# Attention scores in three passes: the lo keys meet only the hi queries over 64 rows, two blocks side by side on the array's halves

## The chip, the cores and the metric

The kernel runs on one core of a Trainium2 chip. The metric is the device time of one execution in microseconds (us). The engines are PE (TensorE, with its weight loads shown apart as PEld), DVE (VectorE), ACT (ScalarE), POOL (GpSimd) and SP (SyncE, which here issues nearly all DMAs).

## What is computed

One layer of a decoder trunk over a sequence of 1024 positions and a model width of 1024, in float32. Three causal token mixers share one normalised input and one wide input projection:

- branch a, differential attention: 4 heads, each with two score maps (m = 0, 1) over 64-wide queries and keys; the weights are the first softmax less lambda times the second;
- branch b, sliding-window attention: 8 query heads over 2 key heads, a window of 128, a sink per head;
- branch c, forgetting attention: 8 heads, with a decay that is a running sum over positions.

```python
s = jnp.einsum('bqhmd,bkhmd->bhmqk', qblk, k) * scale
p = jax.nn.softmax(s + bias[None, :, None], axis=-1)
w = p[:, :, 0] - lam * p[:, :, 1]
...
s = jnp.einsum('bqhd,bkhd->bhqk', qblk, k) * scale
s = jnp.where((dist >= 0)[None, None], s + decay, -jnp.inf)
p = jax.nn.softmax(s, axis=-1)
```

The first three lines are of branch a, the others of c. Each branch is gated, projected up, merged by sigmoid gates, projected once more and added to the input; a last RMSNorm ends the trunk.

## The kernel before

Every float32 operand of a matmul is kept as two parts, hi (rounded to the format that PE reads, float32r) and lo (the rest), and a product is the sum of the part products.

The work goes in stages. First the input is normalised and the value columns are projected. Then the other projections run in pairs of tiles (`strassen`, lines 160 to 211; its matmuls are lines 109 to 111); queries and keys are split by `spill` (line 417) and written to a scratch tensor in memory, `qd[t, row, s]`, with t = 0 for hi and 1 for lo. The attention stage follows (from line 573), then up-projection and output.

In the attention stage PE's order is written by hand: the loop at line 931 goes through 64 parts (16 of branch b, 32 of c, 16 of a). A part of b is one block of 128 queries; a part of c or a is one group g of two query blocks, i = 2g and 2g + 1, with g going 3, 2, 1, 0 in each head. In each round, the scores of part n (list `sa`) are mixed with the transposes (line 671) and output matmuls (lines 704, 775) of part n - 2 (list `tv`) in proportion to their nominal costs, and after every such piece `fill` puts in filler matmuls: three 512-column matmuls of a gate projection (lines 526 to 528) at a time. The other engines are ordered by a scheduler.

**Scores.** A head's query and key vectors have 64 numbers, so hi and lo stand under each other in 128 rows: `load_q` (line 606) loads hi in rows 0 to 63 and lo in 64 to 127; `load_k` (line 609) loads the hi keys into both halves of one tile and the lo keys into both halves of another. `scores` (line 618) makes a block of up to 512 scores with two matmuls of 128 rows: one gives q_hi k_hi + q_lo k_hi, the other q_hi k_lo + q_lo k_lo. A block is at least 256 wide.

**Score tiles.** Each block goes into a PSUM tile `sc` of one bank; there are two such buffers (BS = 2). VectorE reads it once (line 645 in c and a, line 752 in b: bias, scale and running minimum m into the tile e), followed by a short read of the accumulator. ScalarE then makes the exponentials (lines 651, 755), GpSimd normalises (lines 659, 835).

In `part_c` (line 783) the bias of a group is the tile dk. The odd block is done first; then GpSimd masks 128 columns of dk in place (line 809), and the even block reads the same tile.

**Queues.** SP issues the loads of a part three parts ahead (AHEAD = 3). Query and key tiles share one pool, qk, of NQK = 16 buffers.

Of the kernel before, what the change touches and what calls it, by code (L numbers as in the profile page):

```python
# [32 lines left out]
NST, NW, NSF = 5, 4, 4  # L33
NE, NF, NQK = 6, 3, 16
BP, BS, BT, BY = 2, 2, 2, 2
# [14 lines left out]
def hybrid_block_kernel(ctx, tc, x, norm_gain, w_in, b_forget, lambda_q1, lambda_k1, lambda_q2, lambda_k2,  # L50
# [165 lines left out]
    with tc.tile_pool(name="blk", bufs=8) as blk, \  # L216
# [199 lines left out]
        with tc.tile_pool(name="qkp", bufs=2, reuse_waits="tile") as qkp:  # L416
            def spill(row, scale, c, src):
                hi = qkp.tile([P, 512], F32R, name="qk_hi", bufs=3)
                lo = qkp.tile([P, 512], F32R, name="qk_lo", bufs=3)
                if isinstance(scale, float):  # L420
                    nc.scalar.activation(hi, src, AF.Copy, scale=scale)
                else:
                    nc.scalar.activation(hi, src, AF.Identity, scale=scale)
                nc.vector.scalar_tensor_tensor(lo, src, scale, hi.bitcast(F32), ALU.mult, ALU.subtract)
                for t, v in enumerate((hi, lo)):
                    nc.sync.dma_start(qd[t, row * P:row * P + P, c * 512:c * 512 + 512], v.bitcast(F32))

# [16 lines left out]

            def qk(row, scale):
                return lambda c, src: spill(row, scale, c, src)
            tb.update(hb)
# [43 lines left out]
            for hp in range(4):  # L491
                tiles += [(QC + hp * P, qk(hp, SCALE)), (KC + hp * P, qk(4 + hp, 1.0))]
            tiles += [(QB + t * P, qk(16 + t, qscale_b[:, t:t + 1])) for t in range(4)]
# [79 lines left out]
    with tc.tile_pool(name="at", bufs=2, reuse_waits="tile") as at, \  # L573
# [31 lines left out]

        def load_q(row, m):
            return load_rows(row, m, (0, 1))

# [8 lines left out]

        def scores(xq, kk, i, k0, n):

            ps = ps_s.tile([P, 512], F32, name="sc")  # L620
            q = xq[i // 4][:, (i % 4) * P:(i % 4) * P + P]
            c, o = divmod(k0, 512)
            n = max(n, 256)
            for t in range(2):
                nc.tensor.matmul(ps[:, :n], q, kk[t][c][:, o:o + n], start=t == 0, stop=t == 1)  # L625
            return ps

        def s_cost(n):
            return 2 * max(n, 256) / 2400

        def softmax_rows(xq, kk, i, cuts, bias, scale, tag, done):

# [3 lines left out]

            def chunk(k0, n, last):
                ps = scores(xq(), kk(), i, k0, n)
# [4 lines left out]
                m2 = small.tile([P, 1], F32, name="m")  # L643
                m = st_["m"]
                nc.vector.tensor_tensor_reduce(out=e[:, k0:k0 + n], in0=ps[:, :n], in1=bias(k0, n), op0=ALU.add,  # L645
                                               op1=ALU.min, scale=-scale, scalar=1.0e30 if m is None else m,
                                               accum_out=m2)
                st_["m"] = m2
                if last:
# [4 lines left out]
                    done(e, r, den)  # L654
            ends = cuts[1:] + [L]
            return [(s_cost(z - a), lambda a=a, z=z: chunk(a, z - a, z == L)) for a, z in zip(cuts, ends)]

# [74 lines left out]
        def part_b(u, kv, i):  # L732
# [3 lines left out]

            def score(hh):
                h = 4 * kv + hh
                if hh == 0:
# [7 lines left out]
                ps = ps_s.tile([P, 512], F32, name="sc")  # L747
                q = u["q"][hh][i // 4][:, (i % 4) * P:(i % 4) * P + P]
                for t in range(2):
                    nc.tensor.matmul(ps[:, :2 * P], q, u["k"][t][:, k0:k0 + 2 * P], start=t == 0, stop=t == 1)  # L750
                e = st_["e"][hh // 2][:, hh % 2, :W]
                nc.vector.tensor_tensor_reduce(out=e, in0=ps[:, :W], in1=posB[:, 2 * P - W:], op0=ALU.add,
                                               op1=ALU.min, scale=-SLOPES_B[h], scalar=nsink[:, h:h + 1],
                                               accum_out=m4[:, hh:hh + 1])
                nc.scalar.activation(e, e, AF.Exp, bias=m4[:, hh:hh + 1], scale=-1.0, accum_out=d4[:, hh:hh + 1])
                st_["es"].append(e)
                if hh == 3:
                    s4 = small.tile([P, 4], F32, name="s4")
# [11 lines left out]
            def pv(b):  # L770
# [9 lines left out]
            return ([(0.22, lambda hh=hh: score(hh)) for hh in range(4)], [(0.44, lambda b=b: tr(b)) for b in range(nblk)],  # L780
                    [(0.43, lambda b=b: pv(b)) for b in range(nblk)], lambda: None)

        def part_c(u, hp, hh, g):
# [6 lines left out]
            def prep():  # L790

                if "ck" not in u:
# [30 lines left out]
        def part_a(u, h, g):  # L823
# [14 lines left out]
            for i in (2 * g, 2 * g + 1):  # L838
                L = P * (i + 1)
                for m in range(2):  # L840
                    sa += softmax_rows(lambda m=m: u["q"][m], lambda m=m: u["k"][m], i, [0] if i < 4 else [0, 512],
                                       lambda k0, n, L=L: posA[:, S - L + k0:S - L + k0 + n], SLOPES_A[h],
                                       "a%d" % (m + 1), lambda e, r, d, m=m, i=i: done(m, i, e, r, d))

# [26 lines left out]
        def load_b(u, kv):  # L871
# [4 lines left out]
            for t in range(2):  # L876
# [4 lines left out]
                u["k"].append(k)  # L881
            u["q"] = [load_q(16 + 2 * kv + t, m) for t in range(2) for m in range(2)]

# [262 lines left out]
```

## Time and profile before

| | us |
|---|---|
| three runs of the kernel before | 1195.36, 1203.62, 1210.67 |
| their median | 1203.62 |
| the profiled execution's own time | 1201.41 |
| its span, first to last instruction | 1199.3 |
| PE busy | 1155.8 |
| DVE busy | 798.9 |
| POOL busy | 688.9 |
| ACT busy | 591.9 |

The profile is of one execution on one core. Busy time is the time covered by an engine's instructions; the record of a matmul reaches into the next one, so PE's busy time shows where PE stood still, not its rate. The rate is read from the starts in a timeline. A row of a group gives busy time, the mean of one instruction, and after the bar the idle time before them with what ended it.

### The profile page before, as it was taken

To read this page: it belongs to the slowest core of one execution; us is meant where nothing else is said; L and a number is where in the kernel's file an instruction comes from. 1 tells how busy PE (TensorE), PEld (TensorE's weight loads), DVE (VectorE), ACT (ScalarE), POOL (GpSimd) and SP (SyncE) were. 2 spreads that over 40 slices of the span, in tenths; PEclk is the share of its full clock that TensorE was granted. 3 is DMA by queue.
4 is the path that set the end of the run, shared out by engine and by line. 5 is a ranking of instruction groups with operands and counts; after the bars stand their busy time and mean duration, and the time that the engine had idled before them with its cause. 6 is when DMAs were issued, how large, how long until landed. Compare 5 with 4: busy or idle time off the path is not lost. (4 is left out here: it accounts for less than half of the span.)

```text
span 1199.3 us, 18793 instructions
## 1 busy us (share of the span) xinstructions
PE 1155.8 (96%) x5787; PEld 977.3 (81%) x5787; DVE 798.9 (67%) x1655; ACT 591.9 (49%) x1255; POOL 688.9 (57%) x684
## 2 busy tenths in 40 slices
PE   7999999999999999999999999999998999989997
PEld 6999878878778788887888888888877778878885
DVE  7667786766775774321887766767766835564897
ACT  6432334333443443332886666667876842334433
POOL 5056585665754754454555666665767632377652
PEclk8999999999999999999999999999999999999999
DMA  7442386675854643338945465456567359897332
GB/s 242 159 154 80 112 283 201 216 246 158 257 192 138 221 132 106 114 97 244 272 131 173 145 195 176 130 174 174 171 209 221 122 169 325 270 333 299 141 119 92
DMA packets 184531, 221.70 MB, mean 185 GB/s; under 512 B 16280, under 2 KB 116712, under 8 KB 182640
## 3 DMA queue, kind: packets, MB, share of 16 engines
q1 hardware_dynamic: 184288, 219.99, 58.2%
q8 instruction: 46, 0.75, 0.3%
q10 hardware_dynamic: 144, 0.52, 0.1%
q14 instruction: 53, 0.43, 0.1%
HBM read 144.89 MB, written 75.56 MB: 184 GB/s over the span
## 5 line engine op out<-in xcount | busy, mean ns | idle before, releaser
L104 POOL TENSOR_TENSOR w_lo<-w_st,w_hi 128x512 fp32r<-128x512 f32 x130 | 175.4, 1352 | 109.5 <-ACT w_hi L101 99.0
L104 POOL TENSOR_TENSOR w_lo<-w_sf,w_hi 128x512 fp32r<-128x512 f32 x96 | 137.8, 1440 | 107.4 <-ACT w_hi L101 100.6
L111 PE MATMUL pm<-t,w_lo 128*128 128x512 f32 x320 | 128.7, 402 | 5.4 <-POOL w_lo L104 5.4
L109 PE MATMUL pm<-t,w_hi 128*128 128x512 f32 x320 | 128.5, 402 | 2.5 <-ACT w_hi L101 2.5
L110 PE MATMUL pm<-t,w_hi 128*128 128x512 f32 x320 | 127.6, 399 | 0.0
L625 PE MATMUL sc<-qk 128*128 128x512 f32 (+2 forms) x384 | 102.4, 358 | 4.4 <-DVE m L645 3.8
L101 ACT CAST w_hi<-w_sf 128x512 fp32r<-128x512 f32 x96 | 58.9, 616 | 57.5 <-PE pm L110 51.4
L678 DVE TENSOR_TENSOR pt<-tp,pt 128x512 fp32r<-128x512 f32 x102 | 70.1, 687 | 23.5 <-ACT pt L677 22.7
L101 ACT CAST w_hi<-w_st 128x512 fp32r<-128x512 f32 x86 | 52.4, 617 | 62.0 <-PE pm L110 51.1
L111 PEld LDWEIGHTS pm<-t,w_lo 128*128 128x128 f32 x320 | 61.2, 191 | 21.5 <-POOL w_lo L104 7.1
L625 PEld LDWEIGHTS sc<-qk 128*128 128x128 f32 x384 | 64.9, 190 | 16.3 <-DVE m L645 6.8
L109 PEld LDWEIGHTS pm<-t,w_hi 128*128 128x128 f32 x320 | 61.2, 191 | 17.7 <-ACT w_hi L101 3.7
L110 PEld LDWEIGHTS pm<-t,w_hi 128*128 128x128 f32 x320 | 61.4, 192 | 14.5
L677 ACT CAST pt<-tp 128x512 fp32r<-128x512 f32 x102 | 59.4, 583 | 20.1 <-PE tp L671 18.8
L167 DVE TENSOR_TENSOR w_sf<-w_st 128x512 f32<-128x512 f32 x40 | 43.7, 1093 | 36.0 <-DMA w_st<-in_w_in_dram 21.8
L659 POOL TENSOR_SCALAR e_c<-e_c,r 128x1024 f32<-128x1024 f32 (+3 forms) x64 | 47.9, 748 | 24.5 <-DVE r L653 20.1
L651 ACT ACTIVATE e_c<-e_c,m 128x1024 f32<-128x1024 f32 (+3 forms) x64 | 49.9, 780 | 16.0 <-DVE m L645 15.1
L704 PE MATMUL y<-pt,v 128*128 128x256 f32 x336 | 55.4, 290 | 2.1 <-DVE pt L678 1.8
L651 ACT ACTIVATE e_a<-e_a,m 128x896 f32<-128x896 f32 (+7 forms) x64 | 49.6, 776 | 14.9 <-DVE m L645 14.4
L835 POOL TENSOR_TENSOR e_a<-e_a,e_a 128x896 f32<-128x896 f32 (+7 forms) x32 | 47.6, 1490 | 15.3 <-ACT e_a L834 15.1
L704 PEld LDWEIGHTS y<-pt,v 128*128 128x128 f32 x336 | 48.0, 189 | 6.8 <-DVE pt L678 3.2
L104 POOL TENSOR_TENSOR pwl<-ws,pwh 128x512 fp32r<-128x512 f32 x28 | 40.7, 1455 | 19.9 <-ACT pwh L101 14.2
(299 smaller groups left out, 3467.5 us busy)
## 6 DMA issues: line engine op xcount, KB each, us to landing
w_st<-in_w_in_dram SPq DMA_DIRECT2D x126, 256.0 KB, 3.3
qk<-qd SPq DMA_DIRECT2D x224, 128.0 KB, 3.0
wo<-wod SPq DMA_DIRECT2D x14, 1024.0 KB, 9.3
row<-gmd SPq DMA_DIRECT2D x48, 256.0 KB, 5.1
qd<-qk_hi SPq DMA_DIRECT2D x42, 256.0 KB, 4.2
qd<-qk_lo SPq DMA_DIRECT2D x42, 256.0 KB, 3.8
vd<-vt SPq DMA_DIRECT2D x24, 384.0 KB, 2.3
v<-vd SPq DMA_DIRECT2D x9, 1024.0 KB, 8.2
```

The lines of the kernel that those rows point to most:

```text
L101: nc.scalar.copy(hi, src)
L104: return eng.tensor_tensor(lo, src, hi.bitcast(F32), ALU.subtract)
L109: nc.tensor.matmul(ps, w[0][:, k, :], r[0][:, k, :], start=start and k == 0, stop=False)
L110: nc.tensor.matmul(ps, w[0][:, k, :], r[1][:, k, :], start=False, stop=False)
L111: nc.tensor.matmul(ps, w[1][:, k, :], r[0][:, k, :], start=False, stop=stop and k == n - 1)
L625: nc.tensor.matmul(ps[:, :n], q, kk[t][c][:, o:o + n], start=t == 0, stop=t == 1)
L651: nc.scalar.activation(e[:, :L], e[:, :L], AF.Exp, bias=m2, scale=-1.0, accum_out=den)
L659: nc.gpsimd.tensor_scalar(out=e, in0=e, scalar1=r, scalar2=1.0, op0=ALU.mult, op1=ALU.mult)
L677: nc.scalar.copy(pt[:, 0, a:], tp[:, a:])
L678: nc.vector.tensor_tensor(pt[:, 1, a:], tp[:, a:], pt[:, 0, a:].bitcast(F32), ALU.subtract)
L704: nc.tensor.matmul(y[:, :256], l_, r_, start=t == 0 and n == 0, stop=last and n == len(mms) - 1)
L835: nc.gpsimd.tensor_tensor(e1[:, :L], e1[:, :L], e2[:, :L], ALU.add)
```

## The change

- In the changed kernel a score job has a first matmul over 128 rows (the query's hi and lo by hi keys) and a second one over 64 rows: the lo keys by the hi query alone. The product of lo query and lo key is left out.
- `scores` takes two jobs. It makes the two first passes, then the second pass of job 0 on rows 0 to 63 and of job 1 on rows 64 to 127. For this, job 1's query has lo above and hi below (`turn`): in a and b the load of map m = 1 swaps the parts; in c the spill already swaps them for odd blocks of 128 positions, with two DMAs of 512-byte pieces in place of one.
- Blocks come in pairs (`paired`): in b two heads, in a the two maps of one query block, in c the even and the odd query block of one head. The nominal costs are the sums of the two, so the loop that mixes the lists sees pieces twice as long.
- In a, the lo keys of both maps are loaded as one tile of 128 rows for each half of the sequence.
- In c, the even block's mask is made ahead in a tile of its own, dg, and a block that reaches over the mask is read by VectorE in two instructions.
- NQK goes from 16 to 15. BS stays 2.

```diff
-NE, NF, NQK = 6, 3, 16
+NE, NF, NQK = 6, 3, 15
...
-            def spill(row, scale, c, src):
+            def spill(row, scale, c, src, turn=False):
...
-                    nc.sync.dma_start(qd[t, row * P:row * P + P, c * 512:c * 512 + 512], v.bitcast(F32))
+                    dst = [qd[n, row * P:row * P + P, c * 512:c * 512 + 512] for n in (t, 1 - t)]
+                    if not turn:
+                        nc.sync.dma_start(dst[0], v.bitcast(F32))
+                    for o in range(2 if turn else 0):
+                        to, fr = (a.rearrange("p (b o e) -> p b o e", o=2, e=P)[:, :, o, :]
+                                  for a in (dst[o], v.bitcast(F32)))
+                        nc.sync.dma_start(to, fr)
...
-                tiles += [(QC + hp * P, qk(hp, SCALE)), (KC + hp * P, qk(4 + hp, 1.0))]
+                tiles += [(QC + hp * P, qk(hp, SCALE, True)), (KC + hp * P, qk(4 + hp, 1.0))]
...
-        def load_q(row, m):
-            return load_rows(row, m, (0, 1))
+        def load_q(row, m, turn=False):
+            return load_rows(row, m, (1, 0) if turn else (0, 1))
...
-        def scores(xq, kk, i, k0, n):
-
-            ps = ps_s.tile([P, 512], F32, name="sc")
-            q = xq[i // 4][:, (i % 4) * P:(i % 4) * P + P]
+        def scores(jobs):
...
+            pss = [ps_s.tile([P, 512], F32, name="sc") for _ in jobs]
+            for ps, (q, kh, kl, n) in zip(pss, jobs):
+                nc.tensor.matmul(ps[:, :n], q, kh, start=True, stop=False)
+            for j, (ps, (q, kh, kl, n)) in enumerate(zip(pss, jobs)):
+                r = slice(64 * j, 64 * j + 64)
+                nc.tensor.matmul(ps[:, :n], q[r], kl[r], start=False, stop=True)
+            return pss
+
+        def job(xq, kk, i, k0, n):
             c, o = divmod(k0, 512)
             n = max(n, 256)
-            for t in range(2):
-                nc.tensor.matmul(ps[:, :n], q, kk[t][c][:, o:o + n], start=t == 0, stop=t == 1)
-            return ps
+            return (xq[i // 4][:, (i % 4) * P:(i % 4) * P + P],) + tuple(kk[t][c][:, o:o + n] for t in range(2)) + (n,)
...
+                o = 0
+                for w, b in bias(k0, n):
+                    m2 = small.tile([P, 1], F32, name="m")
+                    m = st_["m"]
+                    nc.vector.tensor_tensor_reduce(out=e[:, k0 + o:k0 + o + w], in0=ps[:, o:o + w], in1=b, op0=ALU.add,
+                                                   op1=ALU.min, scale=-scale, scalar=1.0e30 if m is None else m,
+                                                   accum_out=m2)
+                    st_["m"] = m2
+                    o += w
...
+        def paired(first, second):
+
+            def both(a, b):
+                for f, ps in zip((a[2], b[2]), scores([a[1](), b[1]()])):
+                    f(ps)
+            return [(a[0] + b[0], lambda a=a, b=b: both(a, b)) for a, b in zip(first, second)]
...
+                dg = st_["dg"] = at.tile([P, P], F32, name="dg", bufs=2)
+                nc.gpsimd.affine_select(out=dg, in_=dk[:, q0:q0 + P], pattern=[[-1, P]],
+                                        compare_op=ALU.is_ge, fill=NEG, base=0, channel_multiplier=1)
...
-                if i == 2 * g + 1:
-
-                    dk = st_["dk"]
-                    nc.gpsimd.affine_select(out=dk[:, q0:q0 + P], in_=dk[:, q0:q0 + P], pattern=[[-1, P]],
-                                            compare_op=ALU.is_ge, fill=NEG, base=0, channel_multiplier=1)
...
+            def biases(i, k0, n):
+                dk = st_["dk"]
+                if i % 2 or k0 + n <= q0:
+                    return [(n, dk[:, k0:k0 + n])]
+                return [(q0 - k0, dk[:, k0:q0])] * (q0 > k0) + [(P, st_["dg"])]
...
-            sa = []
-            for i in (2 * g + 1, 2 * g):
-                sa += softmax_rows(lambda: u["q"], lambda: u["k"], i, [0] if i < 4 else [0, 512],
-                                   lambda k0, n: st_["dk"][:, k0:k0 + n], 1.0, "c", lambda e, r, d, i=i: done(i, e, r))
...
+            even, odd = (softmax_rows(lambda: u["q"], lambda: u["k"], i, lambda k0, n, i=i: biases(i, k0, n), 1.0, "c",
+                                      lambda e, r, d, i=i: done(i, e, r)) for i in (2 * g, 2 * g + 1))
+            sa = paired(even, odd)
...
-                u["q"][m] = load_q(8 + h, m)
-                u["k"][m] = load_k(12 + h, m)
+                u["q"][m] = load_q(8 + h, m, m == 1)
+                u["k"][m] = [load_rows(12 + h, m, (0, 0))]
+            lo = [None, None]
+            for c in (1, 0):
+                lo[c] = at.tile([P, 512], F32R, name="qk", tag="qk", bufs=NQK)
+                nc.sync.dma_start(lo[c].bitcast(F32), qd[1, (12 + h) * P:(13 + h) * P, c * 512:c * 512 + 512])
```

The change moves instructions on PE and VectorE. In the rows that follow, a line number is that of the kernel the rows are of; behind the arrow stand the moving operand (for scores the keys) and the weights (the queries); tile numbers tell buffers apart, and the last number is the shape of the output.

The first place is on PE, at the first group of branch c (head 0, g = 3). Before, a block's two passes follow each other, and other work stands between the first block and the second:

```order
L625 MATMUL sc_6313<-qk_6054,qk_6045 128x512
L625 MATMUL sc_6313<-qk_6060,qk_6045 128x512
L775 MATMUL y_6293<-pt_6269,v_5027 128x512 x2
L625 MATMUL sc_6325<-qk_6051,qk_6045 128x512
L625 MATMUL sc_6325<-qk_6057,qk_6045 128x512
L526 MATMUL pj_6309<-h00h_87,w_hi_6115 128x512
L527 MATMUL pj_6309<-h00l_88,w_hi_6115 128x512
L528 MATMUL pj_6309<-h00h_87,w_lo_6116 128x512
L671 MATMUL tp_6341<-ident_80,eb_6152 128x128 x2
L671 MATMUL tp_6341<-ident_80,eb_6153 128x128 x2
```

Now:

```order
L631 MATMUL sc_6337<-qk_6070,qk_6061 128x512
L631 MATMUL sc_6338<-qk_6070,qk_6061 128x512
L634 MATMUL sc_6337<-qk_6076,qk_6061 128x512
L634 MATMUL sc_6338<-qk_6076,qk_6061 128x512
L798 MATMUL y_6313<-pt_6284,v_5043 128x512 x2
L533 MATMUL pj_6333<-h00h_87,w_hi_6126 128x512
L534 MATMUL pj_6333<-h00l_88,w_hi_6126 128x512
L535 MATMUL pj_6333<-h00h_87,w_lo_6127 128x512
L694 MATMUL tp_6358<-ident_80,eb_6176 128x128 x2
L694 MATMUL tp_6358<-ident_80,eb_6177 128x128 x2
```

The four matmuls of a pair stand together, the two half passes at line 634 next to each other; the output matmuls (775, now 798), the fillers and the transposes (671, now 694) that stood between single blocks now all stand behind the pair.

The second place is on PE in the last head of branch a, where the second chunk of query block 4 is followed by the first chunk of block 5. Before:

```order
L625 MATMUL sc_9786<-qk_9196,qk_9190 128x256
L625 MATMUL sc_9786<-qk_9202,qk_9190 128x256
L625 MATMUL sc_9795<-qk_9217,qk_9208 128x512
L625 MATMUL sc_9795<-qk_9223,qk_9208 128x512
L526 MATMUL pj_9701<-h01h_89,w_hi_9691 128x512
L527 MATMUL pj_9701<-h01l_90,w_hi_9691 128x512
L528 MATMUL pj_9701<-h01h_89,w_lo_9692 128x512
L625 MATMUL sc_9804<-qk_9214,qk_9208 128x256
L625 MATMUL sc_9804<-qk_9220,qk_9208 128x256
L625 MATMUL sc_9817<-qk_9199,qk_9190 128x512
L625 MATMUL sc_9817<-qk_9205,qk_9190 128x512
```

Now:

```order
L631 MATMUL sc_9851<-qk_9268,qk_9262 128x256
L631 MATMUL sc_9852<-qk_9280,qk_9274 128x256
L634 MATMUL sc_9851<-qk_9286,qk_9262 128x256
L634 MATMUL sc_9852<-qk_9286,qk_9274 128x256
L631 MATMUL sc_9873<-qk_9271,qk_9262 128x512
L631 MATMUL sc_9874<-qk_9283,qk_9274 128x512
L634 MATMUL sc_9873<-qk_9288,qk_9262 128x512
L634 MATMUL sc_9874<-qk_9288,qk_9274 128x512
L533 MATMUL pj_9763<-h11h_93,w_hi_9759 128x512
L534 MATMUL pj_9763<-h11l_94,w_hi_9759 128x512
L535 MATMUL pj_9763<-h11h_93,w_lo_9760 128x512
```

Before, a filler group or output matmuls stood behind every second block; now two pairs follow each other with no other matmul between them, and a filler group stands behind the second.

The third place is on VectorE, in the same group of branch c as the first: the reading of the last chunk of the even block (512 to 895 of its columns). ISA is the reading of a score tile and, with m alone, of the accumulator. Before:

```order
L645 ISA e_c_6352,m_6353<-sc_6349,dk_6220 128x512
L645 ISA m_6353 128x1
L678 TENSOR_TENSOR pt_6346<-tp_6341,pt_6346 128x512
L653 RECIPROCAL r_6332<-den_6330 128x1
L645 ISA e_c_6352,m_6364<-sc_6361,dk_6220,m_6353 128x384
L645 ISA m_6364 128x1
L678 TENSOR_TENSOR pt_6399<-tp_6394,pt_6399 128x512
```

Now:

```order
L660 ISA e_c_6343,m_6372<-sc_6366,dk_6236,m_6344 128x256
L660 ISA m_6372 128x1
L660 ISA e_c_6343,m_6374<-sc_6366,dg_6241,m_6372 128x128
L660 ISA m_6374 128x1
L660 ISA e_c_6346,m_6381<-sc_6367,dk_6236,m_6347 128x512
L660 ISA m_6381 128x1
L669 RECIPROCAL r_6378<-den_6376 128x1
```

The 384 columns of the even block, one reading before, are read as 256 with the bias dk and 128 with the mask dg; the odd block's reading, which came before the even block's, stands behind them.

## Rows read from the trace of the kernel before

**Rows 1.** The page: busy time of each engine, share of the span, instructions.

```profile
PE 1155.8 (96%) x5787; PEld 977.3 (81%) x5787; DVE 798.9 (67%) x1655; ACT 591.9 (49%) x1255; POOL 688.9 (57%) x684
```

**Rows 2.** Stretches: length, PE, PEld, DVE, ACT, POOL busy; clock, DMA share, GB/s.

```profile
100.00:550.00 450.00, 442.16 (x1930) 362.95 (x1929) 286.91 (x338) 170.71 (x292) 274.73 (x200) 0.99 0.55 174
562.00:635.00 73.00, 70.28 (x417) 60.86 (x417) 60.11 (x213) 58.98 (x186) 40.64 (x76) 1.00 0.74 204
635.00:855.00 220.00, 217.30 (x1335) 189.95 (x1334) 157.49 (x485) 147.29 (x326) 140.23 (x213) 1.00 0.58 168
855.00:975.00 120.00, 110.91 (x653) 93.22 (x651) 79.48 (x271) 90.71 (x208) 82.61 (x81) 0.99 0.56 168
```

**Rows 3.** Timeline of PE in branch c: start us, length us, line, matmul.

```profile
706.50 0.39 PE L526 MATMUL pj<-h10h,w_hi 128*128 128x512 f32 x1
...
706.96 0.40 PE L528 MATMUL pj<-h10h,w_lo 128*128 128x512 f32 x1
707.20 0.63 PE L704 MATMUL y<-pt,v 128*128 128x256 f32 x4
707.67 0.97 PE L625 MATMUL sc<-qk 128*128 128x384 f32 x4
```

**Rows 4.** Timeline of PE around a sums matmul (line 862).

```profile
847.59 0.52 PE L625 MATMUL sc<-qk 128*128 128x384 f32 x2
847.95 0.40 PE L862 MATMUL pj<-y,ones 128*2 128x256 f32 x2
848.18 0.68 PE L625 MATMUL sc<-qk 128*128 128x512 f32 x2
```

**Rows 5.** Timeline of PE's weight loads in branch c.

```profile
702.37 0.46 PEld L671 LDWEIGHTS tp<-ident,e_c 128*128 128x128 f32 x4
702.80 0.19 PEld L526 LDWEIGHTS pj<-h10h,w_hi 128*128 128x128 f32 x1
```

**Rows 6.** Groups of matmuls by line and shape: busy us, mean ns, idle before.

```profile
L625 PE MATMUL sc<-qk 128*128 128x512 f32 x192 | 62.1, 406 | 4.4 <-DVE m L645 3.8 <-DMA qk<-qd 0.5
...
L625 PE MATMUL sc<-qk 128*128 128x256 f32 x128 | 26.8, 291 | 0.0
...
L750 PE MATMUL sc<-kb,qk 128*128 128x256 f32 x128 | 25.9, 292 | 2.7 <-DMA qk<-qd 1.7 <-DVE m L752 1.1
...
L625 PE MATMUL sc<-qk 128*128 128x384 f32 x64 | 16.9, 344 | 0.0
```

**Rows 7.** Timeline of PE in branch a.

```profile
900.85 1.04 PE L625 MATMUL sc<-qk 128*128 128x512 f32 x2 [2.81 <-DVE m L645]
901.68 0.63 PE L704 MATMUL y<-ptz,v 128*128 128x256 f32 x2
```

**Rows 8.** Timeline of VectorE in the same stretch.

```profile
900.11 0.68 DVE L645 CUSTOM_DVE_ANT_0 e_a<-sc,posA 128x512 f32<-128x512 f32 x1
...
901.93 0.69 DVE L645 CUSTOM_DVE_ANT_0 e_a<-sc,posA 128x512 f32<-128x512 f32 x1 [0.48 <-PE sc L625]
```

**Rows 9.** Groups of VectorE by line and shape, 562 to 975 us.

```profile
L645 DVE CUSTOM_DVE_ANT_0 e_a<-sc,posA 128x512 f32<-128x512 f32 x40 | 27.4, 686 | 4.2 <-PE sc L625 3.4 <-POOL w_hi L103 0.2
...
L645 DVE DVE_READ_ACCUMULATOR2_ANT m<- 128x1 f32 x192 | 15.8, 82 | 0.1
...
L645 DVE CUSTOM_DVE_ANT_0 e_a<-sc,posA,m 128x256 f32<-128x256 f32 x8 | 3.9, 482 | 2.4 <-PE sc L625 1.9
...
L645 DVE CUSTOM_DVE_ANT_0 e_c<-sc,dk,m 128x128 f32<-128x128 f32 x8 | 2.8, 350 | 1.1 <-POOL e_c L659 0.5 <-PE sc L625 0.3
```

**Rows 10.** Who waited for whom: us in total, times, longest us.

```profile
DVE e_c L645 <- POOL dk L809: 4.1, 2, 3.1
...
ACT qk_hi L421 <- DMA qd<-qk_lo: 4.2, 2, 2.7
```

**Rows 11.** The page, DMA issues: count, KB each, us to landing.

```profile
qd<-qk_hi SPq DMA_DIRECT2D x42, 256.0 KB, 4.2
```

More of the change, by code (lines that the diff above doesn't have):

```diff
@@ L443, in sigm, with qk @@
                 return put
-            def qk(row, scale):
-                return lambda c, src: spill(row, scale, c, src)
+            def qk(row, scale, turn=False):
+                return lambda c, src: spill(row, scale, c, src, turn)
             tb.update(hb)
@@ L616, in load_v, with softmax_rows, chunk @@
             return v
-        def scores(xq, kk, i, k0, n):
-            ps = ps_s.tile([P, 512], F32, name="sc")
-            q = xq[i // 4][:, (i % 4) * P:(i % 4) * P + P]
+        def scores(jobs):
[7 more added lines that the diff above has]
+        def job(xq, kk, i, k0, n):
             c, o = divmod(k0, 512)
             n = max(n, 256)
-            for t in range(2):
-                nc.tensor.matmul(ps[:, :n], q, kk[t][c][:, o:o + n], start=t == 0, stop=t == 1)
-            return ps
+            return (xq[i // 4][:, (i % 4) * P:(i % 4) * P + P],) + tuple(kk[t][c][:, o:o + n] for t in range(2)) + (n,)
         def s_cost(n):
             return 2 * max(n, 256) / 2400
-        def softmax_rows(xq, kk, i, cuts, bias, scale, tag, done):
+        def softmax_rows(xq, kk, i, bias, scale, tag, done):
             L = P * (i + 1)
             st_ = {"m": None}
-            def chunk(k0, n, last):
-                ps = scores(xq(), kk(), i, k0, n)
+            def chunk(ps, k0, n, last):
                 if k0 == 0:
@@ L642, in chunk @@
                 e = st_["e"]
[L643 to L648, printed above, removed]
+                o = 0
[7 more added lines that the diff above has]
+                    o += w
                 if last:
@@ L654, in chunk @@
                     done(e, r, den)
-            ends = cuts[1:] + [L]
-            return [(s_cost(z - a), lambda a=a, z=z: chunk(a, z - a, z == L)) for a, z in zip(cuts, ends)]
+            return [(s_cost(min(512, L - k0)), lambda k0=k0: job(xq(), kk(), i, k0, min(512, L - k0)),
+                     lambda ps, k0=k0: chunk(ps, k0, min(512, L - k0), k0 + 512 >= L)) for k0 in range(0, L, 512)]
+        def paired(first, second):
[3 more added lines that the diff above has]
+            return [(a[0] + b[0], lambda a=a, b=b: both(a, b)) for a, b in zip(first, second)]
         def normalise(e, r):
@@ L735, in part_b, with score @@
             st_ = {}
-            def score(hh):
-                h = 4 * kv + hh
-                if hh == 0:
+            def score(pr):
+                if pr == 0:
                     st_["m"] = small.tile([P, 4], F32, name="m4")
@@ L746, in score @@
                 k0 = max(i - 1, 0) * P
[L747 to L757, printed above, removed]
+                pss = scores([(u["q"][2 * pr + j][i // 4][:, (i % 4) * P:(i % 4) * P + P],)
+                              + tuple(u["k"][t][:, k0:k0 + 2 * P] for t in range(2)) + (2 * P,) for j in range(2)])
+                for j, ps in enumerate(pss):
+                    hh = 2 * pr + j
+                    h = 4 * kv + hh
+                    e = st_["e"][pr][:, j, :W]
+                    nc.vector.tensor_tensor_reduce(out=e, in0=ps[:, :W], in1=posB[:, 2 * P - W:], op0=ALU.add,
+                                                   op1=ALU.min, scale=-SLOPES_B[h], scalar=nsink[:, h:h + 1],
+                                                   accum_out=m4[:, hh:hh + 1])
+                    nc.scalar.activation(e, e, AF.Exp, bias=m4[:, hh:hh + 1], scale=-1.0, accum_out=d4[:, hh:hh + 1])
+                    st_["es"].append(e)
+                if pr == 1:
                     s4 = small.tile([P, 4], F32, name="s4")
@@ L779, in pv @@
                               yd["b"].rearrange("(h e) s -> e h s", e=64)[:, 4 * kv:4 * kv + 4, i * P:(i + 1) * P])
-            return ([(0.22, lambda hh=hh: score(hh)) for hh in range(4)], [(0.44, lambda b=b: tr(b)) for b in range(nblk)],
+            return ([(0.44, lambda pr=pr: score(pr)) for pr in range(2)], [(0.44, lambda b=b: tr(b)) for b in range(nblk)],
                     [(0.43, lambda b=b: pv(b)) for b in range(nblk)], lambda: None)
@@ L839, in part_a @@
                 L = P * (i + 1)
[L840 to L843, printed above, removed]
+                sa += paired(*[softmax_rows(lambda m=m: u["q"][m], lambda m=m: u["k"][m], i,
+                                            lambda k0, n, L=L: [(n, posA[:, S - L + k0:S - L + k0 + n])], SLOPES_A[h],
+                                            "a%d" % (m + 1), lambda e, r, d, m=m, i=i: done(m, i, e, r, d))
+                               for m in range(2)])
             def lhs(kb):
@@ L881, in load_b @@
                 u["k"].append(k)
-            u["q"] = [load_q(16 + 2 * kv + t, m) for t in range(2) for m in range(2)]
+            u["q"] = [load_q(16 + 2 * kv + t, m, m == 1) for t in range(2) for m in range(2)]
         vc = {}
@@ L896, in load_a @@
             for m in range(2):
-                u["q"][m] = load_q(8 + h, m)
-                u["k"][m] = load_k(12 + h, m)
+                u["q"][m] = load_q(8 + h, m, m == 1)
[4 more added lines that the diff above has]
+                nc.sync.dma_start(lo[c].bitcast(F32), qd[1, (12 + h) * P:(13 + h) * P, c * 512:c * 512 + 512])
+            for m in range(2):
+                u["k"][m].append(lo)
         parts = []
```

## Prediction

> **What bounds the kernel now.** I read the busy shares first: TensorE is busy 1155.8 of 1199.3 us, VectorE 799 [rows 1]. Since a share is a mean over stages, the second view is the table by stretch. The change sits in the attention stage: branch b (562 to 635 us), c (635 to 855) and a (855 to 975). There PE is busy 96, 99 and 92% of the stretch, VectorE 82, 72 and 66%, ScalarE 81, 67 and 76%; the granted clock is 1.00 to 0.99, the 2.4 GHz level [rows 2]. So PE sets the time, but in b not by much, and what a matmul costs there must be read from start to start, since records overlap.
>
> That is the third view, the timeline. A 512-column matmul starts 0.233 us after the one before it (three from 706.50 to 707.20), four of 256 columns take 0.47 us, 0.118 each [rows 3], two of 384 take 0.36 us, so 0.18 each [rows 4]: about 0.456 ns a column. The record of one lasts longer, 0.40 us for 512 columns; its last 0.17 us lie under the next one. Weights are loaded for each matmul; a run of four loads takes 0.43 us, 0.108 each [rows 5], so a load hides under any matmul of 256 columns.
>
> The score groups have 192 + 64 + 128 matmuls at line 625 and 128 at line 750 [rows 6]: 512 in 256 tiles, two passes each over 128 rows. What PE waits for there is small: 3.8 us and 1.1 us on VectorE's reading of a score tile [rows 6].
>
> **The second pass on halves.** The removed term is the lo-query by lo-key product; the second pass then needs 64 rows, and two tiles' second passes stand on rows 0 to 63 and 64 to 127. The changed order has 128 pairs, with the same 256 first passes and 256 half passes. If both halves run at once, a pair costs three passes for four, and saves the shorter of its two: in 64 pairs 256 columns (0.118), in 24 pairs 384 (0.176), in 40 pairs 512 (0.233). The widths follow from the code: b has 32 pairs of 256; each of c's eight heads has 256, 384, 512 with 256, and 512 with 384; each of a's four heads has 256 four times, 384 twice and 512 six times. Sum: 7.6 + 4.2 + 9.3 = **21.1 us saved**, 1.8% of 1199. Everything else on PE stays: the same number of fillers, transposes and output matmuls.
>
> Two costs of the half passes are not in the trace, since every matmul there uses 128 rows.
>
> First, two half loads must come in ahead of the second pair of passes. Under a 512 or 384 pass two loads of 0.108 nearly fit; under a 256 pass (0.118) up to 0.10 sticks out, times 64 pairs: 0 to 6.4 us. I take 2, since runs of loads in rows 5 go by without a gap and half loads go to different rows.
>
> Second, the array changes its shape twice a pair, 256 times. The nearest row is the sums matmul at line 862, with 2 weight columns in place of 128: it starts 0.36 us after two 384-column matmuls, its two take 0.23 us and the next 512 starts on time [rows 4]. So narrowing the columns cost nothing; narrowing the rows is bounded by nothing and by an array that empties first, 0.17 us each time, 256 x 0.17 = 43.5 us. I take 0, the row's value, and keep the other end as a rival. The Trainium skill ("TensorEngine Tiling (Array Packing)", Key Properties) says that changing the tiling mode drains TensorE, and counts 128x32 among the modes. The matmuls at line 862 show no such drain; for 64 rows no run here shows it. By the page's rule the sum would be that of the second rival below.
>
> **Two score tiles, two buffers.** There are two PSUM buffers for scores before and after. Before, tile n waits for VectorE's reading of tile n-2: one reading, with a tile and other work between. Now both buffers are filled by one pair, both readings start when the pair ends, and the next pair needs both. The price from rows: a matmul's end lies 0.17 after the next could start; VectorE picks up 0.04 later (PE record 900.85 + 1.04 = 901.89, reading at 901.93 [rows 7, 8]); a reading of 512 takes 0.69, its accumulator read 0.08 [rows 9]; PE starts 0.06 after the reading's end (900.79, then 900.85). Needed until the second buffer: 0.17 + 0.04 + 0.69 + 0.08 + 0.69 + 0.06 = 1.73 us, less the 0.23 in which the next pair's first tile runs: **1.50 us of other PE work between pairs**; 1.28 for 384, 1.1 to 1.2 for 256. Before, one reading needed 0.96.
>
> The order, priced with the starts above, gives the work between pairs: in branch a none at two of 48 places (the second fence shows one), one filler group of 0.70 at nine, 1.03 to 1.40 at six more; short by 9.8 us in sum. In c 11 of 48 are short (six of them have 1.17 where 1.50 is needed), 2.9 us; in b 4, 3.0 us. That is 15.8 us; the same count over the order of before gives 2.7 us, so 13.1 more, with VectorE free at once. It is not: at 66 to 82% busy, half a 0.69 instruction stands in front about three times in four, 0.25 us. With that the sums are 25.2 and 5.4, so 19.9 more; and 5.4 agrees with the 3.8 + 1.1 = 4.9 us that the trace of before has [rows 6]. I take the middle, **16.5 us lost**, mostly in a. Queued behind a waiting score matmul is everything on PE, fillers too, so the wait is on the path.
>
> **The pieces of c.** The even tile no longer waits for the odd one's mask: its mask goes into a tile of its own (dg), and its last stretch is read in two instructions at two of four groups per head, 16 more instructions of about 0.35 + 0.08 us [rows 9], 6.9 us of VectorE. A third of c's pairs have no room: 2 us on PE. What goes is VectorE's 4.1 us wait for POOL's mask [rows 10]; VectorE isn't the bound, so 0.
>
> **DMAs.** Eight of the 42 qd<-qk_hi writes, and eight lo ones, become two each with 512-byte pieces. They lie between 100 and 550 us, where the DMA engines are 55% busy and PE 98% [rows 2], and land in 4.2 us [rows 11]. Their only reader is the attention stage. What they hold up is the qk_hi buffer, for which ScalarE waited 4.2 us in all [rows 10]: between 0 and 16 x 4.2 = 67 us if each landing were doubled and bare, taken at 0 by the wait row. In branch a the lo keys of both maps come in two whole tiles, 24 DMAs fewer; the score matmuls waited 1.7 + 0.5 us for loads [rows 6], so 0 to -2.2, taken as 0. The pool has one buffer fewer (15); in the order the later loads still stand over 12 us of PE work ahead of their use. SP and POOL queues get no new wait.
>
> **Sum**, on the profiled execution (1201.4 us): -21.1 + 2 + 16.5 + 2 = -0.6, so **1201 us**. The median of the three runs is 1203.6, their spread 1195 to 1211, so the profiled run stands 0.2% below the median. 2% (24 us) is about what a measurement of this kernel can tell from no change.
>
> **Rivals.**
> 1. VectorE keeps up, because PE's delays give it room to empty its queue and shortages don't add. For it: VectorE idles 28 to 34% in c and a. Against: the shortages in a are of the order, not of the queue. Gain whole: 1201.4 - 21.1 = 1180 us. Chance 0.12.
> 2. Changing from 128 to 64 rows and back empties the array. Place: both ends of each half pass; price up to 0.17 each, 43.5 us, less 0.17 at the 32 short places where the readings run meanwhile (5.4): 1201 + 38 = 1239 us, slower by 3%. It decides the sign from about 0.1 us a change (26 us). For it: 64 rows are a shape that no row shows. Against: line 862. Chance 0.13.
> 3. The change doesn't do what it says: the halves follow each other. Nothing is saved, the waits stay: 1201.4 + 16.5 + 2 = 1220 us. For it: before has no two matmuls at once. Against: they use different rows, different score tiles. Beside this: the Trainium skill ("TensorE: Matmul & The Clock Gate", Part 3) has matmuls of different row groups start some 4 ns apart, and four 32-row tiles 3.07 times as fast; no run here shows it yet. Chance 0.13.
>
> **How the numbers follow.** The forecast has 0.62. Its own range is 1187 to 1213: waits from 7 (13 less 6 that PE's other waits give back) to 24 (a queue of 0.5 us), pieces 0 to 3, loads 0 to 6. Faster by over 2% (below about 1179) needs the first rival and some luck in the loads: 0.05. Slower by over 2% (above about 1227): most of the second rival, a little of the third: 0.16. Within: 0.79. The range to hold 8 in 10 takes in most of rivals 1 and 3 and a part of 2: 1181 to 1230.
>
> **What would show it.** Right: the two half matmuls of a pair start within some 20 ns of each other, and the next matmul 0.23 us later for 512; the score lines' idle time for VectorE's m rises from 4.9 to over 15 us, most of it in a, and PE's share there falls under 92%. Wrong: half matmuls 0.1 us or more behind the first pass (rival 2), a full pass apart (rival 3), or waits for m still near 5 us (rival 1). If the stretch before 550 us has grown, my zero for the DMAs was wrong.

## The result, and the profile after

| | us |
|---|---|
| kernel after, median of four runs | 1253.03 (1245.07 to 1258.49) |
| kernel before, median of four runs | 1205.36 (1195.36 to 1210.67) |
| ratio | 1.0422, interval 1.0378 to 1.0465 |
| the profiled execution of after | 1245.07, span 1243.3 |

The change makes the kernel 4.2% slower. The forecast was 1201 us with a range up to 1230, so the time lies outside it. The second rival, an array that empties at each change of shape (1239 us, chance 0.13), comes nearest, but emptying is only half of what a change of shape costs here, and the change of shape is only a part of the loss.

Where did the time go? First the table by stretch, for the part before the attention stage and then for the branches b, c and a. A border in the prediction has to be mended for this: it let branch a begin at 855 us [rows 2], but the first score matmul of a stands at 811.7. That touched no term of its sum. With the right borders the kernel before reads (length, busy time of PE, PEld, DVE, ACT, POOL with counts, granted clock, DMA share, GB/s):

```profile
562.00:636.00 74.00, 71.28 (x423) 61.72 (x423) 60.35 (x214) 59.98 (x190) 40.75 (x76) 1.00 0.74 203
636.00:812.00 176.00, 173.52 (x1081) 152.41 (x1080) 123.82 (x371) 113.03 (x252) 113.01 (x186) 1.00 0.56 166
812.00:976.00 164.00, 154.17 (x902) 130.20 (x901) 112.90 (x382) 123.96 (x277) 110.31 (x107) 0.99 0.58 171
```

and the kernel after:

```profile
100.00:550.00 450.00, 443.34 (x1944) 363.43 (x1944) 288.27 (x335) 169.17 (x291) 277.13 (x203) 1.00 0.57 177
556.00:643.00 87.00, 83.43 (x423) 63.09 (x422) 60.45 (x213) 61.30 (x189) 41.31 (x78) 0.96 0.61 170
643.00:842.00 199.00, 191.14 (x1078) 146.56 (x1078) 126.66 (x403) 111.73 (x253) 111.79 (x184) 0.99 0.50 147
842.00:1023.00 181.00, 168.48 (x904) 123.95 (x903) 112.72 (x383) 124.94 (x277) 108.52 (x106) 0.98 0.47 145
```

Branch b takes 13 us more, c 23, a 17: 53 in all. Before the stage nothing has grown (it begins at 556 in place of 562 us), and what follows it is 3 us shorter, so the spans of the two profiled executions differ by 44. The ratio gives 51: the profiled execution of after lies 8 us under the median of the four, with a mean granted clock of 0.985 where the others have 0.978 to 0.982. In the stage the records show PE the same number of matmuls but for one (2405 and 2406), and "busy" 96, 96 and 93% of the three stretches, against 96, 99 and 94% before. PE stands idle for 24 us of them, 15 before; so most of the 53 is not idle time, its matmuls start further apart. As in the prediction, that shows only in a timeline. PE around one pair of branch a (start, length, line, tile, shapes, count):

```profile
981.11 0.63 PE L631 MATMUL sc<-qk 128*128 128x512 f32 x2
981.67 0.50 PE L634 MATMUL sc<-qk 64*128 64x512 f32 x2
982.11 0.50 PE L533 MATMUL pj<-h10h,w_hi 128*128 128x512 f32 x1
982.44 0.40 PE L534 MATMUL pj<-h10l,w_hi 128*128 128x512 f32 x1
982.67 0.40 PE L535 MATMUL pj<-h10h,w_lo 128*128 128x512 f32 x1
```

The two first passes take 0.56 us until the halves start, where two 512-column matmuls take 0.47 [rows 3]: 0.09 more. Both halves together take 0.44 until the next matmul, 0.21 more than the 0.233 of one pass (0.20 in the median of the 512-column pairs and of the 256-column ones), and the two halves of a pair start 3 ns apart. The first filler matmul behind them takes 0.33 (to 982.44), 0.10 more; the next takes 0.23 again. By the medians a visit to the half shape costs 0.09 + 0.20 + 0.10 = **0.39 us**; 128 visits cost 50 us, and the 21.1 us that the halves save don't pay for it.

The timeline of the weight loads says what the 0.10 are. Here around a pair of c, whose second tile had to wait for its buffer (0.28):

```profile
749.31 0.19 PEld L631 LDWEIGHTS sc<-qk 128*128 128x128 f32 x1 [0.28 <-DVE m L660]
749.73 0.19 PEld L634 LDWEIGHTS sc<-qk 64*128 64x128 f32 x2 [0.24 <-issue]
750.16 0.19 PEld L533 LDWEIGHTS pj<-h00h,w_hi 128*128 128x128 f32 x1 [0.24 <-issue]
750.26 0.19 PEld L534 LDWEIGHTS pj<-h00l,w_hi 128*128 128x128 f32 x1
750.50 0.19 PEld L535 LDWEIGHTS pj<-h00h,w_lo 128*128 128x128 f32 x1
```

with PE in the same stretch:

```profile
748.87 0.94 PE L631 MATMUL sc<-qk 128*128 128x512 f32 x2
749.73 0.49 PE L634 MATMUL sc<-qk 64*128 64x512 f32 x2
750.16 0.50 PE L533 MATMUL pj<-h00h,w_hi 128*128 128x512 f32 x1
750.50 0.40 PE L534 MATMUL pj<-h00l,w_hi 128*128 128x512 f32 x1
```

The load for line 534 starts at 750.26, 0.24 before its matmul, under the one at line 533. The loads of line 634 and of line 533 behind it start together with their own matmuls, at 749.73 and 750.16: a load is not pulled ahead over a change of shape, and the 0.10 is that bare load, a load with no matmul running over it. All 256 half loads of this trace start within 0.01 us of their matmul, and so do the loads of all 86 fillers behind a pair. So each change costs 0.09 in which nothing new starts, and 0.10 of load.

The Trainium skill ("TensorEngine Tiling (Array Packing)", Key Properties) says that a change of tiling mode drains TensorE; the trace agrees, with 0.09 us of it at each change (called emptying from here on), and shows the bare load beside it. The Trainium skill ("TensorE: Matmul & The Clock Gate", Part 3) lets matmuls on different rows start some 4 ns apart; here it is 3 ns.

The waits in the stage, PE's and its loads' (total us, times, longest); the answer to [rows 6]:

```profile
PEld sc L634 <- issue: 19.7, 63, 0.7
PEld pj L533 <- issue: 12.5, 52, 0.4
PEld sc L631 <- DVE m L660: 11.7, 27, 1.0
PEld y L727 <- DVE pt L701: 8.2, 17, 0.8
...
PE pj L888 <- ACT gr L539: 4.5, 2, 4.2
...
PE y L727 <- DVE pt L701: 3.9, 11, 0.5
PE sc L631 <- DVE m L660: 3.8, 11, 0.7
```

The wait of PE for VectorE's m, 3.8 us and 1.4 at the tiles of b, is hardly longer than before (3.8 and 1.1). But a record of PE lasts 0.17 us beyond the point where the next matmul can start, and the loads show more: 11.7 + 2.4 us, where the kernel before has

```profile
PEld sc L625 <- DVE m L645: 6.8, 10, 3.0
...
PEld sc L750 <- DVE m L752: 1.7, 3, 0.6
```

The rows "<- issue" at lines 634 and 533 are the loads that wait for nothing but the change of shape. Two more rows of after matter below. GpSimd, at the line that builds the next dk, now waits long for VectorE's readings of score tiles, which also read the old dk:

```profile
POOL dk L820 <- DVE m L660: 59.4, 20, 6.3
```

The same line of the kernel before waits 7.9 us for them, and the in-place mask, which the change takes out, 14.4:

```profile
POOL dk L809 <- DVE m L645: 14.4, 13, 2.9
...
POOL dk L797 <- DVE m L645: 7.9, 5, 2.4
```

And PE stands 4.2 us at one sums matmul of branch a (line 888) until ScalarE has copied a filler's result (gr). That copy stands in ScalarE's queue behind an operand of the next stage (yg_b), which waits for VectorE's gate, and the gate for its load:

```profile
ACT yg_b L101 <- DVE gate L569: 5.2, 6, 3.6
...
DVE gate L569 <- DMA gate<-yd_b: 2.5, 2, 2.1
```

In the kernel before the wait of the sums matmuls for gr is 0.3 us in all.

In this one execution the granted clock was 0.61 from 560 to 565 us and 0.71 from 565 to 570 (of 2.4 GHz, so between its two levels), just after PE had stood waiting at b's first pairs; the kernel before has 1.00 there. By these rows I estimate (0.39 + 0.29) x 5 = 3.4 us of the 13 in b. Behind the wait for gr it was 0.70 (955 to 960 us).

### The profile page after: what moved, and what is told of

Read it like the earlier page. It is cut to its first block, busy times and chain, and to the rows that moved or that the text cites. A ratio compares the mean times of both kernels' runs of the same rounds, so it can differ in the third digit from the quotient of the medians.

```text
span 1243.3 us, 18840 instructions
## 1 busy us (share of the span) xinstructions
PE 1192.6 (96%) x5787; PEld 959.6 (77%) x5787; DVE 810.6 (65%) x1687; ACT 590.7 (48%) x1255; POOL 687.3 (55%) x684
## 5 line engine op out<-in xcount | busy, mean ns | idle before, releaser
L167 DVE TENSOR_TENSOR w_sf<-w_st 128x512 f32<-128x512 f32 x40 | 46.8, 1171 | 41.8 <-DMA w_st<-in_w_in_dram 29.9
L700 ACT CAST pt<-tp 128x512 fp32r<-128x512 f32 x102 | 59.4, 582 | 28.6 <-PE tp L694 26.7
L110 PEld LDWEIGHTS pm<-t,w_hi 128*128 128x128 f32 x320 | 60.5, 189 | 14.1
L667 ACT ACTIVATE e_c<-e_c,m 128x896 f32<-128x896 f32 (+3 forms) x64 | 49.6, 776 | 41.1 <-DVE m L660 41.1
L727 PE MATMUL y<-pt,v 128*128 128x256 f32 x336 | 59.9, 298 | 5.2 <-DVE pt L701 3.9
L103 POOL TENSOR_SCALAR w_hi<-w_st 128x512 fp32r<-128x512 f32 x44 | 27.4, 623 | 66.9 <-PE pj L534 59.4
L631 PE MATMUL sc<-qk 128*128 128x512 f32 (+2 forms) x192 | 60.3, 380 | 4.1 <-DVE m L660 3.8
L820 POOL TENSOR_SCALAR dk<-ck 128x1024 f32<-128x1024 f32 (+3 forms) x32 | 25.8, 806 | 59.7 <-DVE m L660 59.4
L682 POOL TENSOR_SCALAR e_c<-e_c,r 128x896 f32<-128x896 f32 (+3 forms) x64 | 47.7, 750 | 10.4 <-DVE r L669 9.8
```

The lines of the kernel that those rows point to most:

```text
L110: nc.tensor.matmul(ps, w[0][:, k, :], r[1][:, k, :], start=False, stop=False)
L167: nc.vector.tensor_tensor(t, x, y, op)
L631: nc.tensor.matmul(ps[:, :n], q, kh, start=True, stop=False)
L667: nc.scalar.activation(e[:, :L], e[:, :L], AF.Exp, bias=m2, scale=-1.0, accum_out=den)
L682: nc.gpsimd.tensor_scalar(out=e, in0=e, scalar1=r, scalar2=1.0, op0=ALU.mult, op1=ALU.mult)
L700: nc.scalar.copy(pt[:, 0, a:], tp[:, a:])
```

## The experiments

Each kernel is a version of one of the two; ratios are against the kernel before, run beside them on the same chip (1200.9 us for experiments 1, 2, 4 and 5, 1201.1 for the others).

**1. The pairs, without the halves** (e1_pairs_128rows: after, second pass over 128 rows).

```diff
-                r = slice(64 * j, 64 * j + 64)
-                nc.tensor.matmul(ps[:, :n], q[r], kl[r], start=False, stop=True)
+                nc.tensor.matmul(ps[:, :n], q, kl, start=False, stop=True)
```

> The changed kernel with the second pass of each pair over all 128 rows again, in the same place of the order: no change of the array's shape and nothing saved. The product left out by the changed kernel is computed again in b and c; in a it is computed against the lo keys of the other map, since these lie in the same tile. Theory A (the array's change of shape costs 0.29 to 0.39 us a visit, 37 to 50 us over 128 pairs): 1253 - 43 + 21 = 1231 us, 1224 to 1237. Rival B (the loss is the pairs' waits for VectorE alone, and the late starts round the half passes only hide them): 1253 + 21 = 1274 us. Rival C (the loss comes from the rest of the change): 1253 + 21 = 1274 us as well.

Measured: 1228.1 us, ratio 1.0231 (1.0199 to 1.0262). So the halves account for 1.0422 - 1.0231 = 1.9%, 23 us, although they take 21 us of passes away. The price by the timeline is 50 - 21.1 = 29, 6 more. About 3 of the 6 fit a PE that is held up and so leaves VectorE more room: the score loads wait 16.9 us for m here, 14.1 in after. The rest isn't placed. And 2.3% of loss have nothing to do with the halves. Its timeline shows a pair that is short of a buffer:

```profile
743.31 0.49 PE L693 MATMUL tp<-ident,e_c 128*128 128x128 f32 x3
743.64 1.08 PE L631 MATMUL sc<-qk 128*128 128x512 f32 x2
744.56 0.62 PE L633 MATMUL sc<-qk 128*128 128x512 f32 x2
745.02 0.40 PE L533 MATMUL pj<-h00h,w_hi 128*128 128x512 f32 x1
```

The two first passes take 0.92 in place of 0.47, since the second tile's buffer isn't free (its load waits 0.42 us for VectorE's m); the second passes take 0.46, with no price ahead of them or behind.

**2. The half shape alone** (e3_before_64row_pass: before, with the second pass of each of the 256 blocks over 64 rows, one after the other; the same edit in b).

```diff
-            for t in range(2):
-                nc.tensor.matmul(ps[:, :n], q, kk[t][c][:, o:o + n], start=t == 0, stop=t == 1)
+            nc.tensor.matmul(ps[:, :n], q, kk[0][c][:, o:o + n], start=True, stop=False)
+            nc.tensor.matmul(ps[:, :n], q[:64], kk[1][c][:64, o:o + n], start=False, stop=True)
...
```

> The kernel before, in its own order, with one edit: the second pass of every block over 64 rows (hi query by lo key; the lo by lo product is left out). One change of shape there and back for each of 256 blocks, no pairs, nothing beside each other, nothing saved, loads as before. Theory A: 256 x 0.29 to 0.39 = 74 to 100 us more, 1279 to 1305 us. Rivals B and C: 1205 us, since neither pairs nor the rest of the change are there.

Measured: 1281.65 us, ratio 1.0672 (1.0642 to 1.0703). No pair, no buffer and no mask has changed, the number of columns is the same, and the kernel loses 80.7 us: 0.315 for each of 256 visits. PE around one of them:

```profile
700.94 0.34 PE L624 MATMUL sc<-qk 128*128 128x384 f32 x1
701.21 0.44 PE L625 MATMUL sc<-qk 64*128 64x384 f32 x1
701.58 0.55 PE L671 MATMUL tp<-ident,e_c 128*128 128x128 f32 x3
```

For 0.18 a pass [rows 4] it takes 0.27 and 0.37: again 0.09 at the entry and 0.19 at the exit, and a filler behind a half pass again takes 0.10 more in the median. This shows the shape's price by itself. At 0.39 a visit it would be 100 us; PE's own waits in the stage fall from 14.6 to 3.9 us, which gives about half of the difference back.

**3. Is it the change, or the narrow shape?** (e10_three_half_steps: each block is three half passes, so a pair has three steps of two halves, and no 128-row pass.)

```diff
-            for ps, (q, kh, kl, n) in zip(pss, jobs):
-                nc.tensor.matmul(ps[:, :n], q, kh, start=True, stop=False)
...
+            for step in range(3):
...
+                    r = slice(64 * j, 64 * j + 64)
+                    nc.tensor.matmul(ps[:, :n], q[r], (kl if step else kh)[r], start=step == 0, stop=step == 2)
```

> The changed kernel with three half passes for each block of a pair and no pass over 128 rows: hi query by hi key, and hi query by lo key twice; the product of lo query and hi key is left out. The columns that PE streams are those of the changed kernel (three steps of two blocks side by side), the array still changes its shape twice a pair, but there are three half steps in each visit. Theory A (the price belongs to the change of shape: some 0.09 us of emptying and 0.10 us of a weight load that comes bare, each way): within 15 us of the changed kernel, 1240 to 1265 us, and half passes that follow a half pass start one pass apart. Rival D (every half pass pays to start, whatever stood before it): two more steps of 0.19 us or more for 128 pairs, 49 us or more above it: 1300 us.

Measured: 1255.01 us, ratio 1.0437 (1.0409 to 1.0465), the same as after. Three half steps cost what two passes and one half step cost, since either has one visit. PE and then the loads around a pair:

```profile
724.34 0.96 PE L633 MATMUL sc<-qk 64*128 64x512 f32 x6
725.23 0.74 PE L726 MATMUL y<-ptz,v 128*128 128x256 f32 x4
```

```profile
724.34 0.53 PEld L633 LDWEIGHTS sc<-qk 64*128 64x128 f32 x6 [0.36 <-issue]
725.23 0.53 PEld L726 LDWEIGHTS y<-ptz,v 128*128 128x128 f32 x4 [0.36 <-issue]
```

Six matmuls take 0.89 = 3 x 0.233 + 0.19. By the medians the first step takes 0.335 (its loads are bare), the second 0.235 (its two loads lie under the first). So the narrow shape itself is as fast as the wide one; only the change is paid.

**4 and 5. The pairs, taken apart.** In e7_pairs_in_turn a pair is still one piece of the order, but block 0 has both its passes before block 1, all of 128 rows:

```diff
-            for j, (ps, (q, kh, kl, n)) in enumerate(zip(pss, jobs)):
-                r = slice(64 * j, 64 * j + 64)
-                nc.tensor.matmul(ps[:, :n], q[r], kl[r], start=False, stop=True)
+                nc.tensor.matmul(ps[:, :n], q, kl, start=False, stop=True)
```

> As the run with 128 rows in pairs, but the two blocks of a pair in turn: both passes of the first, then both of the second, so that VectorE can read the first while PE makes the second. Same product changed in a. Theory A: half of the pairs' waits (16 of some 25 us by the order) go: 1215 us, 1210 to 1222. Rival B: if readings that start together cost what the changed kernel lost, 30 us or more under the run with grouped passes. Rival C: the same as that run.

Measured: 1215.0 us, ratio 1.0126 (1.0091 to 1.0161). In e8_single_blocks each block is a piece of its own, in the same sequence as in the pairs:

```diff
...
-            return [(a[0] + b[0], lambda a=a, b=b: both(a, b)) for a, b in zip(first, second)]
+            return [(x[0], lambda x=x: one(x)) for a, b in zip(first, second) for x in (a, b)]
...
```

> The rest of the change alone: pieces of one block again, both passes over 128 rows, but with the spill in two DMAs, 15 buffers, the lo keys of a in one tile, the mask dg with its two readings, and the even and odd blocks of c in turn. Same product changed in a. Theory A: 1205 us, 1200 to 1212. Rival B: the same, 1205. Rival C: 1240 us or more.

Measured: 1209.74 us, ratio 1.0073 (1.0053 to 1.0093), a little more than expected. Between e8 and experiment 1 lie 1.58%, 19 us, the price of the pairs: 12.6 come with the grouped passes, whose readings start together, and 6.4 with pieces twice as long (little more than the noise, as the two intervals touch).

The traces tell the two apart. The score loads wait for m 9.9 us in e8 and 9.8 in e7, but 16.9 in experiment 1: only the grouped passes lengthen the wait for the two buffers. What is new in e7 is the wait of a sums matmul for gr:

```profile
PE pj L886 <- ACT gr L539: 5.6, 2, 5.3
```

where e8 has

```profile
PE pj L884 <- ACT gr L539: 0.3, 1, 0.3
```

All four kernels with pairs have it (4.5 us in after, 5.0 in experiment 1, 6.9 in experiment 3), and none of the five without (0.3 each). So this one wait, behind a load of the next stage, is the likely cause of most of the 6.4. It wasn't shown by a run: that the time would come back if the copy of gr stood earlier in ScalarE's queue was not tried.

**6. What is left in e8: more buffers for the bias of c** (e9_single_blocks_4f: e8 with four F buffers and 13 for queries and keys).

```diff
-NE, NF, NQK = 6, 3, 15
+NE, NF, NQK = 6, 4, 13
```

> The run with single blocks, with a fourth buffer for the tiles that hold dk (and 13 buffers for queries and keys, for room). In that run GpSimd waited 43 us in c for VectorE before it could write the next dk, and stood in the way of the normalising that PE's transposes wait for. Theory E (the even and odd blocks in turn hold dk longer): GpSimd's wait falls under 15 us and the time to 1201 to 1204 us. Rival F (the 16 more readings on VectorE, or the spill): it stays at 1207 to 1212 us. Fewer query and key buffers may cost something: if PE waits for loads, this run tells nothing.

Measured: 1208.89 us, ratio 1.0069 (1.0044 to 1.0094). No gain, the time that the rival named. But the run settles nothing: with fewer query and key buffers PE's score matmuls wait 5.8 us for loads (1.2 in e8), and GpSimd's waiting only moved. In e8 GpSimd waits in branch c

```profile
POOL dk L816 <- DVE m L658: 43.2, 19, 4.8
```

and in e9

```profile
POOL dg L822 <- DVE m L658: 27.0, 11, 4.6
...
POOL dk L816 <- DVE m L658: 19.4, 19, 2.4
```

**7. Blocks one kind after the other, as before** (e13_odd_then_even: e8, but in c all odd blocks' pieces before the even ones, in a one map before the other).

```diff
...
-            sa = paired(even, odd)
+            sa = in_turn(odd) + in_turn(even)
...
```

> The run with single blocks, but one block after the other as in the kernel before: in c the odd block, then the even one; in a one map, then the other. The mask dg, the 16 more readings, the spill, the lo keys of a in one tile and 15 buffers stay. Theory E (the blocks in turn cost it): 1199 to 1204 us. Rival F: 1207 to 1212 us, as with the blocks in turn.

Measured: 1196.11 us, ratio 0.9961 (0.9941 to 0.9981), even below the time that the theory named. So the interleaving of blocks that a pair needs costs 13.4 us even without pairs, in c and a together. GpSimd's wait for VectorE at dk in c falls from 43.2 to 2.8 us; all its waits at that line together fall from 46 to 11. Of PE's waits in the stage these differ most; in e8

```profile
PE y L724 <- DVE pt L698: 6.5, 8, 2.8
PE tp L691 <- POOL e_c L679: 5.6, 5, 2.0
```

and in this kernel

```profile
PE tp L691 <- POOL e_c L679: 1.4, 1, 1.4
...
PE y L724 <- DVE pt L698: 1.1, 2, 0.9
```

9.6 us less: transposes that wait for GpSimd's normalised weights, and output matmuls that wait for the copies of the transposes. All of PE's waits in the stage together fall from 21.2 to 13.7, and the spans of the two profiled executions differ by as much (1199.1 and 1191.7 us; c is 182 us in one and 175 in the other, a 167 and 164). But the profiled execution of e8 lies 8.6 us under the median of its eleven, so the traces show only about half of the 13.4. That these waits follow from GpSimd standing at dk fits, but wasn't shown by itself. This version, with the change's mask tile and key loads and with passes over 128 rows, takes 0.4% less time than the kernel before, the least of all here.

Added up from the ratios, in us of 1201: mask tile, loads and the rest -4.7; blocks in turn +13.4; pairs as one piece +6.4; grouped passes +12.6; halves +22.9. The sum is 50.6, the 4.2% of the result, as it must be, since each term is a difference of two neighbouring runs.

## Why the prediction was wrong

1. **The step that failed** is the change of shape: "I take 0, the row's value", with line 862 as the nearest row. That row has fewer weight columns, and its starts show no drain; the kernel after has fewer weight rows, and pays 0.19 a change. The two are different changes, and the row was no evidence for the second. Of the signs named, the matmul behind the halves shows it: it starts 0.43 us after them, not 0.23. Even the upper end was a little low: 0.17 a change, 43.5 us, counted the emptying alone; measured are 0.09 of emptying and 0.10 of bare load, 50 us. The term beside it, half loads that stick out (0 to 6.4 us, taken at 2), treated loads as always pulled ahead; they are not at these places.
2. **The saving was right.** The halves run at once, 3 ns apart, and cost one pass: the third rival falls. 21.1 us is a count; the steps of experiment 3, two halves in 0.235 us, bear it out, and experiment 1 fits it within 6 us.
3. **The waits for two buffers were within their range** (7 to 24 us, taken at 16.5): the grouped passes cost 12.6. The pairs cost 19 in all, near the 16.5, but that nearness is luck, since the other 6.4 go, by the traces, with the wait for gr, which the sum did not have. The sign that I named for these waits failed: idle time of PE for m above 15 us. PE's row stays at 5.2; the loads' rows have 14.1. Nor did PE's share in a fall under 92%: with the right borders it is 93%, and 94% before. The first rival, a VectorE that keeps up, falls.
4. **"SP and POOL queues get no new wait" was wrong** for POOL. GpSimd's wait for VectorE at dk is 59.4 us over the stage. I had counted the wait that goes (4.1 us of VectorE, [rows 10]) and had not followed GpSimd's own queue: it builds the next dk in a buffer that VectorE still reads, and the order in which the blocks read dk decides how long it stands there (43.2 us in c for experiment 5, 2.8 for 7). The pieces of c were taken at 2 us; the interleaving (in c and a) costs 13, and 8.8 net of what the rest of the change gives. That it costs this much is shown; that it does so through dk is not.
5. **The DMAs at 0 were right**: the stretch to 550 us has PE busy 98.5%, and the stage starts no later.

With 50 for the shape, 19 for the pairs and 8.8 for the rest, less 21.1, the sum is 1201 + 57; the measured 51 says that about 6 of these overlap.

Open: what exactly in the interleaved order costs PE its 13 us, and how much of the loss is clock. Not tried: several pairs in one visit, which would need more score buffers. By the rows, a visit pays 0.39 and a pair saves 0.12 to 0.23, so it needs two pairs of 512, or four of 256, just to break even.

## What to carry to other kernels

A row stands for a new operation only if it shares the property that changes: narrow columns say nothing of narrow rows, and where no row shares it, the far end of the bound deserves more than a small chance. Before packing matmuls on parts of the array, count the changes between shapes, not the columns saved: here each cost 0.19 us, as much as 420 columns at 0.456 ns, so half-array work pays only in long runs. And where the order of blocks changes, follow the queue of each engine that makes their operands or frees their buffers, not only of the engine that sets the time.

## What was not expected of the hardware

Two things. The weight load, hidden under a matmul of 256 columns or more, comes bare at a change of row count, 0.10 us in each direction, on top of the 0.09 of emptying. (It is not the only bare load: in the kernel before, a filler behind a run of 128-column transposes takes 0.315 us in the median, 75 times, where one behind a 256-column matmul takes 0.23.) Within a run of half steps (experiment 3) the loads of both halves are hidden again, with steps 0.235 us apart for 512 columns. And a half pass over 64 rows takes no less time than one over 128: 0.37 - 0.19 = 0.18 us for 384 columns in experiment 2, the time of the wide pass.
